# First stage of a decoder trunk: who sums the shift's modulation products, how many unread products run ahead, and the address of two weight pieces

## The chip, the cores and the metric

The kernel runs on one core of one Trainium2 chip. The metric is the device time of one execution in microseconds (us), taken as the median of several runs. TensorE (PE in the rows) multiplies matrices, VectorE (DVE) and ScalarE (ACT) do elementwise work, GpSimd (POOL) does little here, and SyncE (SP) issues nearly all loads from HBM. Each engine has its own list of instructions, kept in the order in which the program gives them, and waits on semaphores for the others.

## The reference, cut to what matters

A two-layer decoder over 256 tokens with 1024 features, all in fp32. A vector `c` is turned into shift, scale and gate vectors by large "ada" matrices, and each sub-layer works on a normalized and modulated input. The first sub-layer is a SwiGLU feed-forward network of hidden width 2816.

```python
def rms_norm(x, g):
    return x * rsqrt(mean(x * x) + EPS) * g
def modulate(h, shift, scale):
    return h * (1 + scale) + shift
def swiglu(h, w_in, w_out):
    g, u = split(h @ w_in)
    return (silu(g) * u) @ w_out

c_act = silu(c)
mod = c_act @ ada_w[layer] + ada_b[layer]          # 9 vectors of 1024 a layer
sh1, sc1, g1, sh2, sc2, g2, sh3, sc3, g3 = split(mod, 9)
h = modulate(rms_norm(x, norm_g[layer, 0]), sh1, sc1)
x = x + 0.5 * g1 * swiglu(h, ffn_w_in[layer, 0], ffn_w_out[layer, 0])
...                                                # attention, second FFN, second layer
```

## The kernel before

**Layout.** Features lie on the 128 partitions in eight blocks `k` (0 to 7), the 256 tokens along the free axis. `x[k]` is one such block of 128x256.

**Precision by splitting.** Every fp32 weight piece of 128x1024 (`raw`, loaded by SyncE) is split in two fp32r pieces: `cp_part` makes the high part `wh` by a ScalarE copy, `sub_part` makes the low part `wl` = `raw` - `wh` on VectorE. The input is split too, into `HH` and `HL`. `mm3` then does three matmuls for each 128x128 block of weights: `wh`x`HH`, `wl`x`HH`, `wh`x`HL`. There are six buffers for `raw` and `wh` and five for `wl`. A piece that `shift` names lies 16 or 32 elements further into its buffer; the others begin at the buffer's start. The first FFN shifts pieces 16, 18 and 20 by 16, and none of pieces 0 to 15.

**Modulation.** The ada matrices come in units of two blocks of 128x1024 (`ada`, 1 MB each, three buffers). `ada_block` handles one block: VectorE multiplies it by `cact` (silu(c) on every partition) and sums each row with the bias in the same instruction (`tensor_tensor_reduce`, which the trace shows as CUSTOM_DVE_ANT_0 and a short DVE_READ_ACCUMULATOR2_ANT). The result is one column of a modulation vector in `modall`. For a first-stage unit the first block (i = 0) is for the scale, followed by a tiny operation that makes (1 + scale) * g, and the second block (i = 1) is for the shift. After the second, the load of the unit three further on is issued.

**The first stage.** `ffn(0, 0)` begins with a part of its own: piece 2k and piece 2k+1 hold the weight rows of feature block k for 16 blocks of columns, and all eight PSUM banks accumulate over k. For each k after the first the program order is

```python
ada_block()            # scale block of unit k:  VectorE
cp_part()              # wh of piece 2k:         ScalarE
ada_block()            # shift block of unit k:  VectorE
f = make_h(k, kind, m) # ht on VectorE, HH on ScalarE; f makes HL on VectorE
sub_part()             # wl of piece 2k:         VectorE
cp_part()              # wh of piece 2k+1:       ScalarE
f()
sub_part()             # wl of piece 2k+1:       VectorE
...                    # 16 blocks x 3 matmuls on TensorE (tile pf)
```

`make_h` makes `ht` = x * (1 + scale) * g * r, then `HH` = `ht` + shift. In this part the planner (the `InOrder` wrappers, which estimate each engine's time) adds nothing of its own: `mode` is "hold". Behind it `mode` is "run", and casts, subtractions and further `ada_block` calls are put between the matmuls by the estimated times.

**Ahead of it.** The lines under `warm` run once: `warm(n)` issues n products of a matrix of ones that nobody reads; `pc` spreads `c` over the partitions, `sqs` are squares of x, `psn` is their mean, and `rstd_of` makes r from it by one ScalarE activation (`r`) and three VectorE operations (`ra`, `ra`, `r`). The two blocks of unit 0 are summed just before `rstd_of`; six unread products follow `psn`.

All instructions that go through the wrappers carry line 99 in the rows, so they are told apart by their tiles.

Of the kernel before, what the change touches and what calls it, by code (L numbers as in the profile page):

```python
# [13 lines left out]
AF = mybir.ActivationFunctionType  # L14
ALU = mybir.AluOpType
# [88 lines left out]
def trunk(ctx, tc, a, out):  # L104
# [3 lines left out]
    act = InOrder(tc, nc.scalar, 0.13, 1 / 1200)  # L108
    dve = InOrder(tc, nc.vector, 0.08, 1 / 960)
# [8 lines left out]
    def mmbank(name):  # L118
        return pp.tile([P, 512], F32, tag="mm", name=name, bufs=4)

    def sbank(name):
        return pp.tile([P, 512], F32, tag="s", name=name, bufs=2)

    def abank(name):
        return pp.tile([P, 512], F32, tag="ta", name=name)

    def bbank(name):
        return pp.tile([P, 512], F32, tag="tb", name=name)
# [7 lines left out]
    vecs = cp_.tile([P, a["vecs"].shape[1]], F32, name="vecs")  # L136
# [13 lines left out]
    cact = cp_.tile([P, D], F32, name="cact")  # L150
    small = cp_.tile([P, 24], F32, name="small")
# [3 lines left out]
    def mod_col():  # L155
        nmods[0] += 1
        return modall[:, nmods[0] - 1]

    def table(func):
        act.preload_act_table(func)  # L160
# [15 lines left out]
    ada_done = [0]  # L176

    def ada_dma(pieces=1):
        u = len(ada_tiles)
        if u >= len(ada_list):  # L180
            return
        t = ap_.tile([P, 2, D], F32, tag="ada", name="ada")
        sp.t = max(sp.t, dve.t if u >= 3 else 0.0)
        if pieces == 1:
            sp.dma_start(t.rearrange("p a b -> p (a b)"), a["ada"][u])
        else:
            for i in range(2):
                sp.dma_start(t[:, i], a["ada"][u][:, i * D:(i + 1) * D])
        ada_tiles.append(t)

    def ada_block():

        u, i = divmod(ada_done[0], 2)
        if u >= len(ada_list):
            return
        ada_done[0] += 1
        t = ada_tiles[u]
        m, j = ada_list[u][i]
        if m not in mods:
            mods[m] = [mod_col(), None]  # L200
        mt = mods[m][0]
        col = V_ADAB + 2 * u + i
        dve.tensor_tensor_reduce(
            t[:, i], t[:, i], cact, 1.0, vecs[:, col:col + 1], ALU.mult, ALU.add,
            accum_out=mt[:, j:j + 1])
        kind = m[1] % 3 if m[0] != "kv" else m[1]
        if kind != 0 and m[1] != 5:
            if mods[m][1] is None:
                mods[m][1] = mod_col()
            mx = mods[m][1]  # L210
            js = (j, j + 1) if m == (0, 1) else ((j - 3, j + 1) if j % 4 == 3 else None)
            if js is not None:
                js = slice(*js)
                if kind == 1:
                    gc = V_KVN if m[0] == "kv" else V_NORM + (m[0] * 3 + m[1] // 3) * NC
                    dve.scalar_tensor_tensor(
                        mx[:, js], mt[:, js], 1.0, vecs[:, gc + js.start:gc + js.stop],
                        op0=ALU.add, op1=ALU.mult)
                else:
                    dve.tensor_scalar_mul(mx[:, js], mt[:, js], 0.5)  # L220
        if i == 1:
            ada_dma()

    def need(*ms):
        while ada_done[0] < 2 * max(ada_at[m] for m in ms):
# [6 lines left out]
    def win0_of(l, i):  # L232
        return 0 if (l, i) == (0, 0) else 2 * (NG - K0) + 2 * NG * (2 * l + i - 1)
# [29 lines left out]
    shift = {}  # L263
    for (l, i), j in ((0, 0), K0), ((0, 1), 1), ((1, 0), 0), ((1, 1), 1):
        unit = win0_of(l, i) + 2 * (j - (K0 if (l, i) == (0, 0) else 0))
        first = next(p for p, v in enumerate(pieces) if v[0].tensor is a["win"].tensor
                     and v[0].offset == a["win"][unit].offset)
        shift.update({first + p: 16 for p in (0, 2, 4)})
    first = next(p for p, v in enumerate(pieces) if v[0].tensor is a["wlast"].tensor)
    shift.update({p: 16 if p - first in (0, 2, 6) else 32 for p in range(first, len(pieces))})  # L270
    raws, his, los = [], [], []
# [20 lines left out]
    def cp_part():  # L292

        u = len(his)
        n = pieces[u][2]
        act.t = max(act.t, used[u - NHI] if u >= NHI else 0.0)
        raw = raws[u]
        wh = wp.tile([P, WB], F32R, tag="wh", name="wh")[:, shift.get(u, 0):]
        act.plainly(lambda: act.copy(wh[:, :n], raw[:, :n]))
        his.append(wh)  # L300
# [93 lines left out]
    def later(n, f):  # L394
        laters.append([n, f])
# [6 lines left out]
    def mm3(ps, w, xx, first, last):  # L402
        (wh, wl), (xh, xl) = w, xx
        mm(ps, wh, xh, start=first, stop=False, skip_group_check=True)
        mm(ps, wl, xh, start=False, stop=False, skip_group_check=True)
        mm(ps, wh, xl, start=False, stop=last, skip_group_check=True)
        work(P)
# [135 lines left out]
    def ffn(l, i, kind, m, nxt, at=2):  # L543
# [24 lines left out]
        if (l, i) == (0, 0):  # L568
            banks = ([mmbank(f"pf{b}") for b in range(4)] + [sbank(f"pf{b}") for b in range(4, 6)]
                     + [abank("pf6"), bbank("pf7")])  # L570
            for k in range(NC):
                if k:
                    ada_block()
                    cp_part()
                    ada_block()
                f = make_h(k, kind, m)
                sub_part()
                cp_part()
                f()
                sub_part()  # L580
                blk = take("win0")
                for b in range(4 * K0):
                    mm3(banks[b // 2][:, (b % 2) * 256:(b % 2) * 256 + 256], blk(b * P), hn[k],
                        k == 0 and b % 2 == 0, k == NC - 1)
            table(AF.Silu)
            cp_part()
            sub_part()
            cp_part()
            sub_part()
            mode[0] = "run"  # L590
            for j in range(K0):
                if j < 2:
                    evac(banks[2 * j], banks[2 * j + 1])
                    if j == 0:
                        flush()
                        flush()
                else:
                    later(2 * j - 2, lambda j=j: evac(banks[2 * j], banks[2 * j + 1]))
            j0 = K0
        elif kind == "late":  # L600
            banks = [mmbank("lg0"), mmbank("lg1"), sbank("lu0"), sbank("lu1")]
            r = None
            for kh in range(2):
                blk = take("win")
                for kk in range(4):
                    k = kh * 4 + kk
                    for b in range(4):
                        mm3(banks[b][:, :SX], blk(kk * 512 + b * P), hx[k], k == 0, k == NC - 1)
                    if k == 2:
                        r = rstd_of(AF.Silu)  # L610
                        mh = MakeH(r, m)
                    elif 2 < k < 7:
                        mh.go(2 if k < 6 else 1)
            mh.go(2)
            mode[0] = "run"
            sg = kp.tile([P, 512], F32, tag="w512a", name="sg")
            hf = kp.tile([P, 512], F32, tag="w512b", name="hf")
            cols = []

            def late_block(b):  # L620
                if b == 0:
                    cols.append(late_cols(banks))
                c = cols[0]
                t = kp.tile([P, S], F32, tag="sq", name=f"lt{b}")
                dve.tensor_tensor(t, banks[b][:, :S], r, op=ALU.mult)
                cs = slice((b % 2) * S, (b % 2) * S + S)
                if b < 2:
                    act.activation(sg[:, cs], t, AF.Silu, bias=c[:, b:b + 1])
                else:
                    dve.scalar_tensor_tensor(hf[:, cs], t, c[:, b:b + 1], sg[:, cs],  # L630
                                             op0=ALU.add, op1=ALU.mult)
                if b == 3:
                    hid_out(hf)
            for b in range(4):
                later(2 + b, lambda b=b: late_block(b))
            j0 = 1
# [234 lines left out]
    def warm(n):  # L871

        pw = bbank("warm")
        for _ in range(n):
            mm(pw[:, :P], ones, ones, start=True, stop=True)
# [14 lines left out]
    for k in range(0, NC, 2):  # L890
# [3 lines left out]
        if k % 4:  # L894
            i = k // 4
# [1 line left out]
            dve.tensor_tensor(sq4[2 * i], sq4[2 * i], sq4[2 * i + 1], op=ALU.add)  # L897
    table(AF.Abs_reciprocal_sqrt)
    warm(2)
    ada_block()  # L900
    ada_block()
    rstd = rstd_of(None, [sq4[i][:, h * S:(h + 1) * S] for i in (0, 2) for h in range(2)])
    warm(6)
    cp_part()


# [223 lines left out]
    op, rest = attention_a()  # L1130
# [227 lines left out]
    op, rest = attention_b()  # L1358
# [132 lines left out]
```

## Time and profile before

| | |
|---|---|
| median of 3 runs | 986.5 us (986.34 to 987.54) |
| the profiled execution: its own time | 988.11 us |
| its span, first to last instruction | 986.3 us |
| mean granted TensorE clock | 0.996 |
| TensorE busy | 974.8 us (99%) |
| VectorE busy | 807.7 us (82%) |
| ScalarE busy | 552.2 us (56%) |
| moved by DMA | 267.18 MB |

A row of the timeline gives the start in us from the span's start, the duration, the engine, the line, the operation, output and inputs with their shapes, and in brackets the idle time before it with what ended it. A row of the windows gives, for a stretch of the span, its length, the busy time of each engine with the number of instructions, the granted TensorE clock (1.00 is full, 0.50 half), the share of time in which the DMA engines were busy, and GB/s.

### The profile page before, as it was taken

To read this page: it belongs to the slowest core of one execution; us is meant where nothing else is said; L and a number is where in the kernel's file an instruction comes from. 1 tells how busy PE (TensorE), PEld (TensorE's weight loads), DVE (VectorE), ACT (ScalarE), POOL (GpSimd) and SP (SyncE) were. 2 spreads that over 40 slices of the span, in tenths; PEclk is the share of its full clock that TensorE was granted. 3 is DMA by queue.
4 is the path that set the end of the run, shared out by engine and by line. 5 is a ranking of instruction groups with operands and counts; after the bars stand their busy time and mean duration, and the time that the engine had idled before them with its cause. 6 is when DMAs were issued, how large, how long until landed. Compare 5 with 4: busy or idle time off the path is not lost. (4 is left out here: it accounts for less than half of the span.)

```text
span 986.3 us, 20552 instructions
## 1 busy us (share of the span) xinstructions
PE 974.8 (99%) x8164; PEld 951.4 (96%) x8164; DVE 807.7 (82%) x1348; ACT 552.2 (56%) x900; POOL 82.6 (8%) x123
## 2 busy tenths in 40 slices
PE   8999999999999999999999999999999999999996
PEld 7999999998999999999998999999999999999996
DVE  6979979989989999878897998889975698555565
ACT  4466545575777644454675544545566576454431
POOL 0000100000112000000000000000039214300000
PEclk9999999999999999999999999999999999999999
DMA  9987999958776699889958999989795248956641
GB/s 361 414 339 275 328 369 341 354 207 295 279 231 237 210 376 378 299 256 320 335 180 324 322 333 343 334 301 324 277 263 154 94 143 240 251 192 183 188 145 43
DMA packets 67762, 267.18 MB, mean 271 GB/s; under 512 B 8233, under 2 KB 8385, under 8 KB 57554
## 3 DMA queue, kind: packets, MB, share of 16 engines
q1 hardware_dynamic: 64224, 258.31, 74.6%
q0 software_dynamic: 3008, 6.91, 2.4%
q8 instruction: 64, 1.05, 0.4%
q10 hardware_dynamic: 434, 0.64, 0.2%
q14 instruction: 32, 0.26, 0.1%
HBM read 263.70 MB, written 2.65 MB: 270 GB/s over the span
## 5 line engine op out<-in xcount | busy, mean ns | idle before, releaser
L99 DVE TENSOR_TENSOR wl<-raw,wh 128x1024 fp32r<-128x1024 f32 (+1 forms) x360 | 400.0, 1126 | 89.3 <-issue 22.4
L99 ACT CAST wh<-raw 128x1024 fp32r<-128x1024 f32 (+1 forms) x360 | 347.6, 975 | 216.1 <-PE pu L99 94.0
L99 DVE CUSTOM_DVE_ANT_0 ada<-ada,cact,vecs 128x1024 f32<-128x1024 f32 x160 | 203.4, 1278 | 0.2 <-DMA ada<-in_ada 0.2
L99 PE MATMUL pg<-HH,wl 128*128 128x256 f32 x608 | 168.2, 277 | 0.0
L99 PE MATMUL pg<-HH,wh 128*128 128x256 f32 x608 | 168.2, 277 | 0.0
L99 PE MATMUL pu<-HH,wh 128*128 128x256 f32 x608 | 168.1, 276 | 0.0
L99 PE MATMUL pu<-HL,wh 128*128 128x256 f32 x608 | 168.1, 276 | 0.0
L99 PE MATMUL pg<-HL,wh 128*128 128x256 f32 x608 | 168.1, 276 | 0.0
L99 PE MATMUL pu<-HH,wl 128*128 128x256 f32 x608 | 168.0, 276 | 0.0
L99 PE MATMUL po<-hidh,wh 128*128 128x256 f32 x528 | 145.7, 276 | 0.0
L99 PE MATMUL po<-hidh,wl 128*128 128x256 f32 x528 | 145.7, 276 | 0.0
L99 PE MATMUL po<-hidl,wh 128*128 128x256 f32 x528 | 145.7, 276 | 0.0
L99 PEld LDWEIGHTS pg<-HH,wh 128*128 128x128 f32 x608 | 114.1, 188 | 0.7 <-issue 0.6
L99 PEld LDWEIGHTS pg<-HL,wh 128*128 128x128 f32 x608 | 114.2, 188 | 0.0
L99 PEld LDWEIGHTS pu<-HH,wh 128*128 128x128 f32 x608 | 114.2, 188 | 0.0
L99 PEld LDWEIGHTS pg<-HH,wl 128*128 128x128 f32 x608 | 114.1, 188 | 0.0
L99 PEld LDWEIGHTS pu<-HH,wl 128*128 128x128 f32 x608 | 114.1, 188 | 0.0
L99 PEld LDWEIGHTS pu<-HL,wh 128*128 128x128 f32 x608 | 114.1, 188 | 0.0
L99 PEld LDWEIGHTS po<-hidh,wh 128*128 128x128 f32 x528 | 99.1, 188 | 0.0
L99 PEld LDWEIGHTS po<-hidh,wl 128*128 128x128 f32 x528 | 99.1, 188 | 0.0
L99 PEld LDWEIGHTS po<-hidl,wh 128*128 128x128 f32 x528 | 99.1, 188 | 0.0
L99 ACT CAST hidh<-hf 128x512 fp32r<-128x512 f32 x44 | 27.3, 622 | 38.5 <-DVE hf L99 38.5
(235 smaller groups left out, 1887.1 us busy)
## 6 DMA issues: line engine op xcount, KB each, us to landing
raw<-in_win SPq DMA_DIRECT2D x176, 512.0 KB, 6.1
ada<-in_ada SPq DMA_DIRECT2D x79, 1024.0 KB, 7.4
raw<-in_wout SPq DMA_DIRECT2D x48, 384.0 KB, 5.8
raw<-in_wout SPq DMA_DIRECT2D x48, 320.0 KB, 5.4
raw<-in_wqk SPq DMA_DIRECT2D x16, 512.0 KB, 6.2
raw<-in_wo SPq DMA_DIRECT2D x16, 512.0 KB, 5.2
raw<-in_wlast SPq DMA_DIRECT2D x16, 512.0 KB, 3.7
raw<-in_wv SPq DMA_DIRECT2D x8, 512.0 KB, 6.3
```

The source lines that it names most:

```text
L99: return self.tc.keep_in_program_order(f(*args, **kw))
```

## The change

In the first stage the shift's block is taken apart: VectorE only multiplies (a plain `tensor_tensor`), ScalarE sums the product (a copy with `accum_out`) and adds the bias in a second, one-column activation. The shift's block now comes ahead of the scale's. This holds for units 0 to 7; later units go through `ada_block` as before. The unread products between `psn` and the first pieces become ten instead of six. Pieces 2 and 6 are shifted by 16 elements.

```diff
         ada_done[0] += 1
+        ada_one(u, i)
+        if i == 1:
+            ada_dma()
+
+    def ada_pair():
+        u = ada_done[0] // 2
+        ada_done[0] += 2
+        ada_one(u, 1, True)
+        yield
+        ada_one(u, 0)
+        ada_dma()
+        yield
+
+    def ada_one(u, i, on_act=False):
         t = ada_tiles[u]
 ...
         col = V_ADAB + 2 * u + i
+        if on_act:
+            dve.tensor_tensor(t[:, i], t[:, i], cact, op=ALU.mult)
+            s = small[:, 10 + u % 2:11 + u % 2]
+            act.activation(t[:, i], t[:, i], AF.Copy, accum_out=s)
+            act.activation(mt[:, j:j + 1], s, AF.Identity, bias=vecs[:, col:col + 1])
+            return
         dve.tensor_tensor_reduce(
 ...
-        if i == 1:
-            ada_dma()
 ...
+    shift.update({2: 16, 6: 16})
 ...
                 if k:
-                    ada_block()
+                    pair = ada_pair()
+                    next(pair)
                     cp_part()
-                    ada_block()
+                    next(pair)
 ...
     warm(2)
-    ada_block()
-    ada_block()
+    for _ in ada_pair():
+        pass
     rstd = rstd_of(None, [sq4[i][:, h * S:(h + 1) * S] for i in (0, 2) for h in range(2)])
-    warm(6)
+    warm(10)
     cp_part()
```

## The prediction

> **What bounds the kernel now.** I read the cores first, then the waits between 14 and 62 us (the first stage), then the windows around it, then the timelines of VectorE, ScalarE and TensorE there.
>
> ```profile
> core 0: 986.3 us, clock 0.996
> PE 974.8 (99%) x8164; PEld 951.4 (96%) x8164; DVE 807.7 (82%) x1348; ACT 552.2 (56%) x900; POOL 82.6 (8%) x123
> ```
>
> TensorE is busy 99% of the span, so only its rate, its clock and its waits matter. The change touches the first 62 us. Windows there, and one from later for comparison:
>
> ```profile
> 12.19:15.60 3.41, 2.06 (x13) 1.46 (x13) 3.34 (x6) 1.80 (x3) 0.00 (x0) 1.00 0.99 411
> 15.60:19.02 3.42, 3.42 (x19) 3.42 (x18) 3.38 (x7) 1.05 (x1) 0.00 (x0) 0.50 1.02 418
> 22.19:61.76 39.57, 39.57 (x338) 39.57 (x337) 38.23 (x59) 19.50 (x25) 0.00 (x0) 1.00 1.02 414
> 281.85:285.26 3.41, 2.55 (x24) 2.02 (x23) 3.09 (x6) 2.86 (x6) 0.00 (x0) 1.00 0.08 30
> ```
>
> Columns are PE, PEld, DVE, ACT, POOL, then clock, DMA share, GB/s. Two things are seen. After a window in which TensorE was busy 2.06 of 3.41 us, the clock fell to 0.50 for 3.42 us: half of that, 1.7 us, is TensorE time lost. And from 22.19 to 61.76 TensorE never pauses, but VectorE is busy 38.23 of 39.57 us: it is nearly the bound as well. The first and last products of the stage:
>
> ```profile
> 14.16 0.39 PE L99 MATMUL pf<-HH,wh 128*128 128x256 f32 x1 [1.14 <-ACT HH L99]
> 56.11 0.28 PE L99 MATMUL pf<-HH,wh 128*128 128x256 f32 x1
> 61.77 0.27 PE L99 MATMUL pg<-HH,wh 128*128 128x256 f32 x1
> ```
>
> TensorE starts block k = 0 at 14.16, the last block (k = 7) at 56.11 and leaves at 61.77: 5.66 us for 48 products, 0.118 each. Now VectorE, its start and one whole round (k = 1), and the last `HL`:
>
> ```profile
> 8.41 1.28 DVE L99 CUSTOM_DVE_ANT_0 ada<-ada,cact,vecs 128x1024 f32<-128x1024 f32 x1 [0.18 <-DMA ada<-in_ada]
> 9.82 1.28 DVE L99 CUSTOM_DVE_ANT_0 ada<-ada,cact,vecs 128x1024 f32<-128x1024 f32 x1
> 11.64 0.48 DVE L99 SCALAR_TENSOR_TENSOR ra<-psn,eps,r 128x256 f32<-128x256 f32 x1 [0.54 <-ACT r L99]
> ...
> 16.22 1.28 DVE L99 CUSTOM_DVE_ANT_0 ada<-ada,cact,vecs 128x1024 f32<-128x1024 f32 x1
> 17.42 0.08 DVE L99 DVE_READ_ACCUMULATOR2_ANT modall<- 128x1 f32 x1
> 17.54 0.16 DVE L99 SCALAR_TENSOR_TENSOR modall<-modall,vecs 128x1 f32<-128x1 f32 x1
> 17.61 1.28 DVE L99 CUSTOM_DVE_ANT_0 ada<-ada,cact,vecs 128x1024 f32<-128x1024 f32 x1
> ...
> 18.82 0.48 DVE L99 SCALAR_TENSOR_TENSOR ht<-x,modall,r 128x256 f32<-128x256 f32 x1
> 19.22 1.22 DVE L99 TENSOR_TENSOR wl<-raw,wh 128x1024 fp32r<-128x1024 f32 x1
> 20.35 0.48 DVE L99 SCALAR_TENSOR_TENSOR HL<-ht,modall,HH 128x256 fp32r<-128x256 f32 x1
> 20.82 1.23 DVE L99 TENSOR_TENSOR wl<-raw,wh 128x1024 fp32r<-128x1024 f32 x1
> 21.96 1.28 DVE L99 CUSTOM_DVE_ANT_0 ada<-ada,cact,vecs 128x1024 f32<-128x1024 f32 x1
> ```
>
> ```profile
> 54.81 0.48 DVE L99 SCALAR_TENSOR_TENSOR HL<-ht,modall,HH 128x256 fp32r<-128x256 f32 x1
> ```
>
> A VectorE round takes 21.96 - 16.22 = 5.74 us without a hole, against TensorE's 5.66. The last `HL` is ready at 54.81 + 0.48 = 55.29; TensorE needs it for its third product of k = 7, at 56.11 + 2 x 0.118 = 56.35. Allowing 0.05 for the hand-over, VectorE is 1.0 us ahead, and that lead is what the halved clock gave it. ScalarE has room:
>
> ```profile
> 11.13 0.47 ACT L99 ACTIVATE r<-psn,eps 128x256 f32<-128x256 f32 x1 [1.85 <-PE psn L99]
> 11.51 1.03 ACT L99 CAST wh<-raw 128x1024 fp32r<-128x1024 f32 x1
> ...
> 15.88 1.05 ACT L99 CAST wh<-raw 128x1024 fp32r<-128x1024 f32 x1 [0.84 <-DMA raw<-in_win]
> 19.33 0.51 ACT L99 ACTIVATE HH<-ht,modall 128x256 fp32r<-128x256 f32 x1 [2.40 <-DVE ht L99]
> ```
>
> The cast of piece 2 (15.88) is done at 16.93, long before VectorE wants it at 19.22; then ScalarE idles 2.40 us until `ht`. So the casts run ahead of VectorE today, and that is what the change breaks.
>
> **The change part by part.** *The product on VectorE.* A plain 128x1024 product has no row of its own; the nearest is the subtraction `wl` of the same shape: 1.22 us, the next instruction 1.13 after its start. The sum it replaces holds VectorE 18.82 - 17.61 = 1.21. Relief: 0.08 per k. But the scale's block, with its read-out and tiny operation, now comes last, right before `ht`, which needs its result. Today the next sum starts 0.07 after the tiny operation (17.54 to 17.61); `ht` must wait for its end, 0.16 plus some 0.04: 0.13 lost. VectorE alone would need 5.74 - 0.08 + 0.13 = 5.79 a round. It is not relieved at all.
>
> *The sum on ScalarE, and who is queued behind it.* The nearest rows of ScalarE:
>
> ```profile
> L99 ACT ACTIVATE sq<-x 128x256 f32<-128x256 f32 x40 | 16.2, 404 | 1.0 <-POOL acc L441 1.0
> L99 ACT CAST wh<-raw 128x1024 fp32r<-128x1024 f32 x256 | 266.3, 1051 | 146.5 <-PE pu L99 85.1 <-PE po L99 23.9 <-DMA raw<-in_win 10.2
> L99 ACT ACTIVATION_READ_ACCUMULATOR nl<-nl,nm 128x1 f32 x32 | 6.0, 189 | 0.0
> L99 ACT ACTIVATE ssl<-ssl 128x1 f32<-128x1 f32 x2 | 0.6, 295 | 13.6 <-DVE ssl L99 13.6
> 255.00 0.49 ACT L99 ACTIVATE nl<-nl,nm 128x256 f32<-128x256 f32 x1
> 255.40 0.19 ACT L99 ACTIVATION_READ_ACCUMULATOR nl<-nl,nm 128x1 f32 x1
> ```
>
> A copy with a sum over 1024 columns costs what the cast does, 1.04 (0.94 until its read-out starts, by the 0.49 and 0.40 of the last two rows), the read-out 0.19, the one-column activation 0.30, of which 0.20 until the next. In program order they stand ahead of the cast of piece 2k, which cannot run early any more: it waits for the copy, the copy waits for the product, and the product stands on VectorE behind `wl` of piece 2k-1. The `wl` of piece 2k then waits for that cast. That closes a loop through both engines. One round, from product to product: product 1.22, hand-over 0.03, copy 0.94, read-out 0.19, hand-over 0.03, activation 0.20, cast 1.04, hand-over 0.04, then `wl` to `HL` 1.13 (19.22 to 20.35), `HL` to `wl` 0.47, `wl` to the next product 1.14 (20.82 to 21.96). Sum 6.43, against 5.74: 0.69 more per k. VectorE by itself would reach `wl` after 1.13 + 1.21 + 0.12 + 0.20 + 0.40 = 3.06 and is held until 3.69, so it idles some 0.63 a round. Bounds: with an activation of 0.15 and a copy 0.1 shorter 6.2, with 0.3 more on ScalarE 6.7. I take 6.43, whose terms all have near rows.
>
> *The start.* The shift's half comes first now, and it is the half that is loaded second:
>
> ```profile
> 1.64 1.15 SPq L99 DMA_DIRECT2D ada<-in_ada  x2
> ada<-in_ada SPq DMA_DIRECT2D x2, 512.0 KB, 7.0
> ```
>
> The first half ended VectorE's wait at 8.41, 6.8 after its issue at 1.64; with a mean of 7.0 the second took 7.2 to 7.4 after an issue near 2.1, so it is there at 9.3 to 9.5, and at 9.82 at the latest, where it is used today. I take 9.5. Then: product to 10.72, copy, read-out and activation until 12.11 (0.03 + 0.94 + 0.19 + 0.03 + 0.20), and only behind them `r`, whose `psn` is there at 11.13: it ends at 12.58, and `ra` starts at 12.62 instead of 11.64. The start moves by 1.0 us (0.8 to 1.3).
>
> *Ten unread products.*
>
> ```profile
> 10.89 2.13 PE L99 MATMUL warm<-ones 128*128 128x128 f32 x12
> ```
>
> Twelve records for six products take 2.13; eight more take 0.9 to 1.7 at full or half clock, so they end at 13.9 to 14.7. The first `pf` comes at 14.16 + 1.0 = 15.2: they lie wholly in that wait and cost nothing. Whether they keep the next window at full clock is open, for the idle time that they fill is about what the later start adds. Here it hardly matters: TensorE waits for data from k = 1 or 2 on either way, and gets back what a halved window took.
>
> *Two pieces at another address difference.* The nearest rows are pieces 17 and 18, unshifted and shifted by 16:
>
> ```profile
> 64.61:67.33 2.72, 2.72 (x26) 1.00 0.92 337
> 67.34:70.17 2.83, 2.83 (x26) 1.00 0.73 237
> ```
>
> The stage's own pieces take 39.57 / 14 = 2.83 each. So a shifted piece should cost 2.83 still, and the later ones stay at 2.83 or go to 2.72. While TensorE waits for data this is worth nothing; at the end the last two pieces count, 0.2 at most. A loss is not excluded but has no row; I keep 0 to 0.2 and take 0.1.
>
> *Loads.* The same loads in the same order on SyncE's queue, each issued later with the VectorE instruction that frees its buffer. They become less dense, since 2 MB per 6.43 us is 310 GB/s against the 414 of the window row, so they hide.
>
> *The sum.* The third product of k = 7 moves from 56.35 to 55.34 + 1.0 + 7 x 0.69 = 61.2, which is 4.8 later, less 0.1: **+4.7 us**. TensorE is the bound behind the stage and gives nothing back. Against the profiled execution that is 988.11 + 4.7 = 992.8. The runs' median, 986.5, lies 1.6 lower; if part of that is a start without the halved window, those runs are already limited by VectorE's round (1.0 us earlier at k = 7), and the change costs them up to 5.7. That gives 991.2 to 992.2; I say **991.8 us**.
>
> **The rivals.** *The loop doesn't close.* If the cast isn't late (a shorter sum than any row shows), VectorE's own 5.79 a round remains: 55.34 + 1.0 + 7 x 0.05 = 56.7 against 56.35, so +0.4, or +1.4 on runs without the halved window: 986.9 to 987.9, no change that a measurement of this kernel could tell (0.2%, 2 us). For it speaks that ScalarE is idle half the stage (19.50 of 39.57); against it the program order.
>
> *Faster.* TensorE keeps its clock (1.7 us) and twelve pieces run at 2.72 (1.3 us): up to 3 us, 983.5; with VectorE's data as the next limit some 984.5. It decides only if VectorE's round falls below TensorE's 5.66, and if `r` isn't late. Against it: the 5.79 above. The Trainium skill (Perfetto Trace Analysis, Optimizing Scalar/DVE Operations) says that with VectorE saturated, moving work to ScalarE may make sense. By that rule this is the outcome; the rows say that only 0.08 a round moves.
>
> *Slower still.* Waits of 0.7 us per k lower TensorE's clock again, and a halved window at the end adds 1.7: 993.5. For it: the window at 12.19. Against it: the window at 281.85, busy 2.55 of 3.41, stayed at 1.00 with no drop but the two that 0.996 allows (at 15.60 and behind the last product), and TensorE would be busy 5.66 of 6.43, which is 88%. The Trainium skill (TensorE: Matmul & The Clock Gate, the table on why this matters) wants no idle gap above some 3 us; by it these waits could never lower the clock. The trace disagrees: the longest gap before the drop was 1.14 us. So this rival keeps a small chance.
>
> **How the numbers follow.** Forecast 0.74 (own range 990 to 993); no loop 0.11; faster 0.06; slower still 0.06; a loop half as long (0.35 a round, 989.5) 0.03. Faster than 0.2%: 0.06. Within 0.2%: 0.11. Slower: 0.83. The range leaves out the first two rivals and reaches from the half loop to the lower clock: 989.3 to 993.5.
>
> **What would show it.** Right: on VectorE an idle time of some 0.6 us before each even `wl`, ended by ScalarE's `wh`; products about 6.4 us apart; on ScalarE copy, read-out, activation, cast, `HH`, cast in that order; `ra` near 12.6; TensorE waiting 0.7 us before each k, and the first `pg` near 66.5. Wrong: casts of even pieces that run before the copy, a round of 5.8 or less, or a first `pg` before 63.

## The result, and the profile after

The changed kernel takes 1000.39 us (median, 1000.0 to 1000.52), against 986.5 before: 13.9 us more, ratio 1.014 (95% interval 1.0128 to 1.0152). The forecast was 991.8, range 989.3 to 993.5. The direction was right; the time is 6.9 us above the range.

The profiled execution of the changed kernel took 1000.0 us. Its core, from the cores and the page:

```profile
core 0: 997.9 us, clock 0.992
PE 978.3 (98%) x8172; PEld 952.9 (95%) x8172; DVE 809.7 (81%) x1340; ACT 564.3 (57%) x924; POOL 81.8 (8%) x123
```

The span grew by 997.9 - 986.3 = 11.6 us, less than the medians did, since the profiled execution of the kernel before took 988.11 us, 1.6 above its median. It grew in two places. The first is the first stage. VectorE there, with the start, one round and the next product:

```profile
9.64 1.23 DVE L99 TENSOR_TENSOR ada<-ada,cact 128x1024 f32<-128x1024 f32 x1 [1.19 <-DMA ada<-in_ada]
...
12.77 0.48 DVE L99 SCALAR_TENSOR_TENSOR ra<-psn,eps,r 128x256 f32<-128x256 f32 x1 [0.51 <-ACT r L99]
...
17.41 1.22 DVE L99 TENSOR_TENSOR ada<-ada,cact 128x1024 f32<-128x1024 f32 x1
18.55 1.28 DVE L99 CUSTOM_DVE_ANT_0 ada<-ada,cact,vecs 128x1024 f32<-128x1024 f32 x1
...
20.06 0.49 DVE L99 SCALAR_TENSOR_TENSOR ht<-x,modall,r 128x256 f32<-128x256 f32 x1
21.11 1.23 DVE L99 TENSOR_TENSOR wl<-raw,wh 128x1024 fp32r<-128x1024 f32 x1 [0.56 <-ACT wh L99]
22.25 0.48 DVE L99 SCALAR_TENSOR_TENSOR HL<-ht,modall,HH 128x256 fp32r<-128x256 f32 x1
22.65 1.22 DVE L99 TENSOR_TENSOR wl<-raw,wh 128x1024 fp32r<-128x1024 f32 x1
23.78 1.22 DVE L99 TENSOR_TENSOR ada<-ada,cact 128x1024 f32<-128x1024 f32 x1
```

ScalarE in the same round, and TensorE's first product of the stage and first one behind it:

```profile
18.66 1.06 ACT L99 ACTIVATE ada<-ada 128x1024 f32<-128x1024 f32 x1 [2.42 <-DVE ada L99]
19.62 0.19 ACT L99 ACTIVATION_READ_ACCUMULATOR ada<-ada 128x1 f32 x1
19.84 0.29 ACT L99 ACTIVATE modall<-small,vecs 128x1 f32<-128x1 f32 x1
20.05 1.03 ACT L99 CAST wh<-raw 128x1024 fp32r<-128x1024 f32 x1
20.98 0.50 ACT L99 ACTIVATE HH<-ht,modall 128x256 fp32r<-128x256 f32 x1
21.39 1.03 ACT L99 CAST wh<-raw 128x1024 fp32r<-128x1024 f32 x1
```

```profile
15.35 0.38 PE L99 MATMUL pf<-HH,wh 128*128 128x256 f32 x1 [2.69 <-ACT HH L99]
66.59 0.27 PE L99 MATMUL pg<-HH,wh 128*128 128x256 f32 x1
```

This is the loop that was forecast: the cast of piece 2k starts at 20.05 behind copy, read-out and bias activation, and `wl` waits 0.56 for it. A round takes 23.78 - 17.41 = 6.37 us. The stage is left at 66.59 instead of 61.77: 4.82 later.

From there TensorE keeps about that distance (4.5 to 5.0) for 650 us. The second place is the change from the second layer's first FFN to its attention. TensorE before and after:

```profile
721.97 0.28 PE L99 MATMUL po<-hidl,wh 128*128 128x256 f32 x1
722.08 0.28 PE L99 MATMUL lp<-HH,wh 128*128 128x258 f32 x1
```

```profile
726.52 0.28 PE L99 MATMUL po<-hidl,wh 128*128 128x256 f32 x1
731.56 0.58 PE L99 MATMUL lp<-HH,wh 128*128 128x258 f32 x1 [4.75 <-ACT HH L99]
```

Where there was no pause (0.11), the changed kernel pauses 5.04 us, and then runs at half clock (window after: PE, PEld, DVE, ACT, POOL, clock, DMA share, GB/s):

```profile
729.84:736.67 6.83, 5.11 (x21) 4.94 (x22) 2.96 (x5) 2.90 (x5) 2.92 (x4) 0.50 1.02 387
```

At the last `po` the distance to the kernel before is 726.52 - 721.97 = 4.55, behind the pause 731.56 - 722.08 = 9.48, and the halved clock (5.11 busy us at half, at most 2.55 lost) brings it to the 11.6 of the end. Why `HH` was late is read on ScalarE, whose cast of 16 columns of `HH` at 731.30 is what the first `lp` waited for:

```profile
724.48 1.05 ACT L99 CAST wh<-raw 128x1024 fp32r<-128x1024 f32 x1 [2.70 <-DMA raw<-in_wq]
728.31 1.04 ACT L99 CAST wh<-raw 128x1024 fp32r<-128x1024 f32 x1 [2.78 <-DMA raw<-in_wq]
730.35 1.04 ACT L99 CAST wh<-raw 128x1024 fp32r<-128x1024 f32 x1 [1.00 <-DMA raw<-in_wq]
731.30 0.20 ACT L99 CAST HH<-modall 128x16 fp32r<-128x16 f32 x1
732.14 0.51 ACT L99 ACTIVATE HH<-x,modall 128x256 fp32r<-128x256 f32 x1 [0.64 <-DVE x L99]
```

Three casts of `wq` pieces stand ahead of that cast in ScalarE's order and wait for their loads. Those loads had come to a near standstill. The DMA view of 717 to 725 shows it, first of the kernel before, then of the changed one:

```profile
DMA packets 460, 1.56 MB, mean 195 GB/s; under 512 B 81, under 2 KB 81, under 8 KB 460
```

```profile
DMA packets 164, 0.52 MB, mean 65 GB/s; under 512 B 38, under 2 KB 38, under 8 KB 164
raw<-in_wq SPq DMA_DIRECT2D x3, 512.0 KB, 13.2
```

A load of 512 KB takes 13.2 us there. The kernel before has a weaker form of it. One event stands just ahead of the low rate in both traces, the write of the last FFN's gate to HBM, 1024 elements of 4 bytes each at its own place (POOL, before and after):

```profile
715.29 0.96 POOL L716 DMA_DIRECT2D gdram<-modall  x1 [188.47 <-DVE modall L99]
```

```profile
712.90 0.96 POOL L737 DMA_DIRECT2D gdram<-modall  x1 [181.53 <-DVE modall L99]
```

It waits for the last modulation unit. Before, it starts 6.8 us ahead of the first `lp`; after, 13.6 us ahead of the last `po`. So it has moved some 7 us forward against TensorE's work: the units behind the stage are taken earlier. SyncE's queue shows it too: behind the load of the last unit six pieces of `wout` were still to come, now it is ten (before, after):

```profile
693.93 11.77 SPq L99 DMA_DIRECT2D raw<-in_wout  x6
```

```profile
690.84 19.16 SPq L99 DMA_DIRECT2D raw<-in_wout  x10
```

The units are placed by the planner, whose estimates the stage's instructions feed. The write lands 11.3 us after its start in the kernel before (at 726.6) and 10.8 in the changed one (at 723.7), and in both traces the rate of the loads rises again within 1.5 us of that.

### The profile page after: what moved, and what is told of

Read it like the earlier page. It is cut to its first block, busy times and chain, and to the rows that moved or that the text cites. A ratio compares the mean times of both kernels' runs of the same rounds, so it can differ in the third digit from the quotient of the medians.

```text
span 997.9 us, 20600 instructions
## 1 busy us (share of the span) xinstructions
PE 978.3 (98%) x8172; PEld 952.9 (95%) x8172; DVE 809.7 (81%) x1340; ACT 564.3 (57%) x924; POOL 81.8 (8%) x123
## 5 line engine op out<-in xcount | busy, mean ns | idle before, releaser
L99 DVE CUSTOM_DVE_ANT_0 ada<-ada,cact,vecs 128x1024 f32<-128x1024 f32 x152 | 193.1, 1278 | 0.0
```

Source lines behind the costliest of these rows:

```text
L99: return self.tc.keep_in_program_order(f(*args, **kw))
```

## The experiments

Three theories for the second place. **A**: the changed estimates alter the order behind the stage, and that costs it; within it A1: the early gate write starves the `wq` loads, A2: the order of the loads alone. **B**: the delay of 4.8 us itself moves the work into a bad time. To separate estimate and execution, two small functions were added to the wrappers: `plan(f)` lets `f` count in the planner's estimates and issues nothing, `run(f)` issues `f` and counts nothing.

**The changed stage, the old order.**

```diff
-        ada_one(u, 1, True)
+        plan(ada_one, u, 0)
+        plan(ada_one, u, 1)
+        run(ada_one, u, 1, True)
...
-        ada_one(u, 0)
+        run(ada_one, u, 0)
...
-    warm(10)
+    warm(6, 4, run)
```

> The changed first stage runs, but the planner's estimates are fed with the instructions of the stage before, so that the order of everything behind the stage is that of the kernel before. Theory A (the order behind the stage cost the second part): the first pg stays near 66.6, 4.8 later than before, but the 5.0 us wait of TensorE near 726 and the halved clock at 729 to 737 are gone; 991.3 (986.5 + 4.8) to 993.6 (1000.4 - 6.8). Theory B (the delay itself moves the FFN's end into a slow stretch of the memory at a fixed time): all of it stays, about 1000.

Measured: 992.88 us, ratio to before 1.0066 (1.0051 to 1.0081).

```profile
66.38 0.28 PE L99 MATMUL pg<-HH,wh 128*128 128x256 f32 x1
```

The stage ends as in the changed kernel; along all matmuls behind it the distance to the kernel before stays at 4.4 to 4.7, and the pause is gone.

**The old stage, the changed order.** The same the other way round: `plan(ada_one, u, 1, True)` and `run(ada_one, u, 0)`, and so on; pieces 2 and 6 are not shifted here.

> The first stage of the kernel before runs, but the planner's estimates are fed with the changed one's instructions, so that the order behind the stage is that of the changed kernel. Theory A: first pg near 61.8 as before, but a wait of some 5 us of TensorE where the second attention begins (near 720) and a halved clock behind it: 986.5 + 6.8 = 993.3. Theory B: no such wait, 986.5.

Measured: 994.25, ratio 1.0076 (1.0061 to 1.0091).

```profile
ACT wh L99 <- DMA raw<-in_wq: 8.3, 3, 5.2
...
PE lp L99 <- ACT HH L99: 6.6, 1, 6.6
```

These are its waits from 700 to 740 (total, times, longest): a stage as fast as before (its first `pg` is at 60.23), and a pause of 6.6 us. B falls. The two parts, 6.3 and 7.6, add up to the 13.9.

**The gate write later, first form.** POOL's write waits for a VectorE copy late in the last FFN; in the changed kernel and in the one before.

```diff
-                g = mods[self.gate][1]
+                g = cp_.tile([P, NC], F32, name="glate")
+                tc.keep_in_program_order(nc.vector.tensor_copy(g, mods[self.gate][1]))
```

> The changed kernel, with the write of the last FFN's gate to HBM (gdram, 1024 elements of 4 bytes) made to wait for a small VectorE copy late in that FFN; orders as in the changed kernel. Theory A1 (the early write slows the loads of wq): the wq packets stay short at 717 to 725, the casts of wq are on time, the 5.0 us wait is gone: 991.3 to 993.6. Theory A2 (the order of the loads alone, not the write): the wait stays, about 1000. Theory B: about 1000.

> The kernel before with the same late gate write. Theory A1: the slow wq packets at 720 to 726 vanish from there and stand behind the later write; the cast at 726.5, which waited 2.90 for its load, comes earlier, though TensorE had not to wait for it: 986.5, 0 to 1 less. A2 and B: the packets are slow as before, 986.5.

Measured: 1020.07 (ratio 1.0334, 1.0319 to 1.035) and 1014.63 (1.0275, 1.0258 to 1.0292): a miss. The pause at `lp` is gone in the first (its waits from 700 to 745 name no `lp` and no `in_wq`), but TensorE is slower everywhere. The new tile has 32 bytes per partition, and the placement of the built programs shows that everything placed behind it, all weight buffers (`raw`, `wh`, `wl`) but also `ada` and the small temporaries, lies 32 bytes further, while `x`, `HH` and `HL` stay. So the pair said nothing sure on A1, and was repeated without a new tile.

**The gate write later, second form.** The copy goes into unused columns of `small`.

```diff
-                g = mods[self.gate][1]
+                g = small[:, 12:20]
+                tc.keep_in_program_order(nc.vector.tensor_copy(g, mods[self.gate][1]))
```

> The changed kernel with the late gate write again, but the VectorE copy goes into unused columns of an existing tile, so that no address moves. Theory A1 (the early write slows the loads of wq): the matmuls keep their spacing, the wait of TensorE at 726 is gone and the halved clock behind it too, the slow packets stand near 900 behind the write: 1000.4 - 5.0 - 1.7 = 993.7, between 992.5 and 994.5. Theory A2 (the order of the loads alone): about 1000. If the cost of the first late-gate kernels was the lateness of the gate and not the moved addresses: 1010 or more.

> The kernel before with the late gate write in the unused columns. If the 28 us of its first form came from the moved addresses: 985.5 to 986.8, with the wq packets at 0.2 us throughout. If they came from the late write: 1010 or more.

Measured: 992.80 (1.0059, 1.0044 to 1.0074) for the changed kernel, 986.85 (1.0006, 0.9996 to 1.0015) for the one before. A late gate costs nothing. The two forms differ in the new tile alone, so the moved addresses cost 27.3 and 27.8 us. In the changed kernel the loads and the casts of the second attention are on time again (DMA view of 717 to 725; ScalarE):

```profile
DMA packets 635, 2.29 MB, mean 286 GB/s; under 512 B 76, under 2 KB 76, under 8 KB 635
raw<-in_wq SPq DMA_DIRECT2D x4, 512.0 KB, 5.6
```

```profile
721.47 1.04 ACT L99 CAST wh<-raw 128x1024 fp32r<-128x1024 f32 x1
722.93 1.06 ACT L99 CAST wh<-raw 128x1024 fp32r<-128x1024 f32 x1 [0.42 <-ACT wh L99]
724.97 1.06 ACT L99 CAST wh<-raw 128x1024 fp32r<-128x1024 f32 x1 [0.98 <-PE po L99]
```

and the standstill has moved with the write, which now starts at 877.9 (DMA view of 882 to 890):

```profile
DMA packets 134, 0.47 MB, mean 58 GB/s; under 512 B 20, under 2 KB 20, under 8 KB 134
raw<-in_win SPq DMA_DIRECT2D x3, 512.0 KB, 10.9
```

There enough pieces lie ready, and TensorE doesn't wait. The order of the loads is that of the changed kernel, so A2 falls.

**The gate write at its early time, in runs of 32 bytes.**

```diff
-[[1, P], [P, NC]]), g)
+[[NC, P], [1, NC]]), g)
```

The elements then lie in another order in HBM and are read back in it, so this kernel leaves out the right order of the gate in the last update. Its instructions and their sizes stay the same.

> The changed kernel with the gate write at its early time, but each partition's 8 elements side by side in HBM (32 bytes each instead of eight times 4 bytes far apart); the gate's columns are then read back in another order, so that the last update uses permuted gates. If the 4-byte scatter is what slows the wq packets: they stay near 0.2 us behind the write, no wait at 726, 993 to 994. If any small write to HBM does it, or its place in time: about 1000.

Measured: 992.63 (1.0058, 1.0043 to 1.0073).

```profile
712.91 0.58 POOL L737 DMA_DIRECT2D gdram<-modall  x1 [181.54 <-DVE modall L99]
```

```profile
DMA packets 687, 2.48 MB, mean 310 GB/s; under 512 B 81, under 2 KB 81, under 8 KB 687
raw<-in_wq SPq DMA_DIRECT2D x4, 512.0 KB, 6.1
```

The same 4 KB at the same moment, as 128 runs instead of 1024 single elements, and no standstill: it is the scatter, not the write. This write lands 4.9 us after its start instead of 10.8. The Trainium skill (DMA: Bandwidth & Descriptors, Specifications) says that transfers under 512 bytes make the DMA engine read, modify and write. Both forms lie far under that limit, and the trace shows that only the one in single elements disturbed the loads; and the victims were another queue's loads, of which that line says nothing.

**Inside the stage: the cast ahead of the copy**, with the old order behind the stage.

```diff
-        run(ada_one, u, 1, True)
+        rest = []
+        run(ada_one, u, 1, rest)
         yield
+        run(rest[0])
         run(ada_one, u, 0)
```

Here `rest` keeps the copy and the bias activation back until `cp_part` has issued the cast.

> The changed first stage with the order of the kernel before behind it, and the cast of piece 2k put ahead of ScalarE's copy and bias activation. If the cast queued behind the copy closes the loop: the cast runs early again, ht becomes what waits for the bias activation (copy 1.06 + 0.19 + 0.29 behind the product, some 0.4 beyond the scale's block of 1.4), a round of 5.8 to 6.2, first pg at 63 to 65: 988 to 991. If the copy's sum itself is what is late, whatever stands behind it: as the same kernel with the cast behind, 992.9.

Measured: 988.79 (1.002, 1.0011 to 1.003), 4.1 less than with the cast behind. VectorE's round closes without a hole:

```profile
17.48 1.22 DVE L99 TENSOR_TENSOR ada<-ada,cact 128x1024 f32<-128x1024 f32 x1
...
20.14 0.48 DVE L99 SCALAR_TENSOR_TENSOR ht<-x,modall,r 128x256 f32<-128x256 f32 x1
20.54 1.22 DVE L99 TENSOR_TENSOR wl<-raw,wh 128x1024 fp32r<-128x1024 f32 x1
...
23.34 1.22 DVE L99 TENSOR_TENSOR ada<-ada,cact 128x1024 f32<-128x1024 f32 x1
```

5.86 a round. It is the place of the cast in ScalarE's queue that closed the loop, not the copy's length.

**The old start on top of that**: unit 0 by two `ada_block` calls.

```diff
-    for _ in ada_pair():
-        pass
+    ada_block()
+    ada_block()
```

> As the kernel with the cast first, and unit 0 summed on VectorE by two ada_blocks as before. If the start's price is the whole of what ra is later (1.1 us): first pf near 14.2, first pg 1.1 earlier, 988.8 - 1.1 = 987.7. If VectorE's round of 5.86 alone (7 x 0.12 over before) holds the end: the same 987.4 to 987.7 is its lower bound, 986.6 cannot be reached. If the start does not matter: 988.8.

Measured: 987.29 (1.0004, 0.9995 to 1.0012). The start's price is 1.5; what is left over before, 0.6, is within what can be told from nothing.

**The two small parts alone, and both together**, in the kernel before: `shift.update({2: 16, 6: 16})`; `warm(6, 4, run)`; both.

> The kernel before with pieces 2 and 6 shifted by 16, nothing else. If the shift is worth what the prediction gave it (0 to 0.2, since VectorE's round of 5.74 is next): 986.3 to 986.6. If the pieces behind a shifted one run at 2.72 instead of 2.83 and VectorE's lead of 1.0 us is used up: 985.6. If it has a part in the 13.9 us: 987.5 or more.

> The kernel before with ten unread products instead of six, the planner's estimates and the orders unchanged. If the window at 12.19 to 15.60 is then busy enough: no halved clock at 15.60, and up to VectorE's lead of 1.0 us gained: 985.6. If VectorE's data are the limit anyway: 986.5. If the four more delay the first pf: 987 or more, with a first pf behind 14.3.

> The kernel before with ten products and the two shifts, so the change without its sums on ScalarE, orders unchanged. If both are harmless and VectorE is next: 985.5 to 986.5, a version not slower than either. If the change's two small parts cost anything: 987.5 or more.

Measured: 986.49 (1.0001, 0.9992 to 1.001), 986.71 (0.9998, 0.9989 to 1.0006) and 986.40 (0.9997, 0.9988 to 1.0006), beside 986.71 for the kernel before. Neither part costs or gains anything. A window of the kernel with ten products, and the same of the kernel with two shifted pieces and six products:

```profile
15.60:19.02 3.42, 3.42 (x33) 3.42 (x32) 3.38 (x7) 1.05 (x1) 0.00 (x0) 1.00 1.02 418
```

```profile
15.60:19.02 3.42, 3.42 (x32) 3.42 (x31) 3.39 (x8) 1.28 (x2) 0.00 (x0) 1.00 1.01 417
```

The halved window of the kernel before is in neither, so its absence can't be put down to the ten products. From the first `ra` to the first `pg` they take 60.90 - 11.64 = 49.3 us and 60.18 - 11.10 = 49.1, the kernel before with its halved window 61.77 - 11.64 = 50.1. Where no window is halved VectorE's round sets the time, with six products as with ten. No version that measurably beats the kernel before came out of these runs.

## Why the prediction was right and wrong

In medians the steps are: 0.6 for VectorE's longer round and the small parts, 1.5 for the start, 4.1 for the cast behind the copy, 7.5 for the order behind the stage. That is 13.7; the 0.2 up to 13.9 is the difference between two medians of the kernel before (986.5 and 986.71). The prediction had the first three and not the fourth.

Right, step by step. *The loop*: forecast 6.43 a round, measured 6.37; idle 0.6 ahead of the even `wl`, measured 0.56; the order on ScalarE as foretold. *VectorE alone*: forecast 5.79, measured 5.86 with the cast ahead. *The start*: `ra` at 12.62 forecast, 12.77 measured; in medians 1.5 rather than 1.0. *Ten products* and *two pieces*: nothing, as said. First `pg` near 66.5 forecast, 66.59 measured. The stage by itself gives 992.88, inside the range. It is 1.1 above the forecast, most likely because the usual run of the old stage ends earlier than the profiled one did: with two shifted pieces, in an execution of 986.25 us, the first `pg` is at 60.18, and with the changed order behind it at 60.23, not at 61.77. Against 60.18 the 66.38 of the changed stage is 6.2 later, and the medians say 6.3, where the prediction allowed "up to 5.7".

Wrong: the step *Loads*, "The same loads in the same order", and in *The sum* "TensorE is the bound behind the stage and gives nothing back". Both held the program behind the stage for unchanged, so the sum has no term for it, and the runs put 7.5 us there (7.6 with the old stage). The front part of this document says that behind the stage the planner places casts, subtractions and `ada_block` calls by estimated times, and the change alters what these estimates add up to. The order did change, the gate's write came some 7 us earlier against TensorE, and the first weights of the second layer's attention, which nothing else had threatened, came late. The load rate in that step is a little off too, without a bearing on the time: two pieces of 128x1024 and a unit of twice that, 4 bytes each, in 6.43 us are 326 GB/s, not 310.

The rival "slower still" named a halved clock inside the stage, brought about by the 0.7 us waits. The changed kernel has one there, from 16.45 to 19.87, but behind the 2.69 us wait of the start, and it cost little, as the prediction said of that window: the kernel with the late gate has none and reaches its first `pg` at 66.38. The one that cost time came behind the 5.04 us pause. The Trainium skill (TensorE: Matmul & The Clock Gate, the table on why this matters) wants no idle gap above some 3 us: for this pause the trace agrees.

What stays open: why 1024 elements of 4 bytes hold up reads for so many us, where in HBM or in the DMA engines that happens, and why the planner's estimate turns a slower stage into earlier modulation units; the runs only show that the estimates alone do it.

## What to carry to other kernels

Where a planner orders the work, a changed instruction changes its estimates, and with them the order hundreds of microseconds later: compare the orders behind the change, not only the stage. An offloaded operation is paid for by what is queued behind it on the new engine; put it behind the work that others wait for. Write small vectors to HBM in runs, or at a time when enough loads lie ready.

## What the runs showed of the hardware that was not expected

A scatter of 4 KB in 4-byte elements held the loads of another queue at 65 GB/s over 8 us, against 286 to 310 without it; at its later place it was 58, where the changed kernel without it moves 208. How much it takes differs: in the kernel before the same 8 us still had 195.

Moving all weight buffers, and the temporaries behind them, by 32 bytes against `HH` and `HL` costs 27 to 28 us in 990. Which of the moved buffers counts was not tried. TensorE is busy throughout in both, yet of the same stretch of time (first form, then second form of the late gate in the changed kernel) the trace has

```profile
350.00:480.00 130.00, 130.00 (x1098) 130.00 (x1097) 110.61 (x152) 62.06 (x77) 0.00 (x0) 1.00 0.88 311
```

```profile
350.00:480.00 130.00, 130.00 (x1149) 130.00 (x1149) 114.69 (x162) 64.91 (x83) 0.00 (x0) 1.00 0.92 327
```

1098 products against 1149: 0.1184 us each against 0.1131, at full clock in both.

And the clock did not follow the busy share of one window alone. In the kernel before its changes at 15.60, 19.02 and 981.58 lie whole steps of 3.4133 us apart (965.98 is 283 of them), and in the changed kernel so do those at 16.45, 19.87 and 729.84. The steps lie elsewhere in each execution, so a window has to be cut at the steps of its own. In the kernel with the cast first the clock drops at 981.94, behind the last product; 283 such steps ahead of that is 15.97. In the window that ends there TensorE was busy 1.92 us, less than the 2.06 that stand ahead of the halved window in the kernel before, and it kept its full clock:

```profile
12.56:15.97 3.41, 1.92 (x16) 1.53 (x14) 3.02 (x6) 2.29 (x4) 0.00 (x0) 1.00 1.00 411
15.97:19.38 3.41, 3.40 (x27) 3.20 (x28) 3.37 (x4) 1.94 (x3) 0.00 (x0) 1.00 1.00 412
```

What decides between the two was not tried.
